# Gates for two output tiles at a time with the merge of the branches one chunk later, its additions on VectorE

## The chip, the cores and the metric

The kernel runs on one core of one Trainium2 chip. The metric is the device time of one execution in microseconds (us). Everything happens on the core's engines: TensorE (PE in the profile, its weight loads PEld), VectorE (DVE), ScalarE (ACT), GpSimd (POOL), and the queues that issue transfers (SP above all).

## The reference, cut to what matters

The program runs two blocks. The first has two "hybrid" layers, the second two layers of another attention and a mixture of experts. The change is in the first block only, in the step that merges three branches:

```python
def hybrid_layer(x, ...):                        # x: 256 tokens x 1024
    h = rmsnorm(x, norm1_w) * (1 + sc1) + sh1
    u = h @ w_in                                 # 1024 x 5632
    u_pool, u_conv, b_conv, c_conv, q, k, v, gate_logits = jnp.split(u, offsets, axis=-1)
    y_pool = pool_mixer(u_pool, pool_w, pool_scale)
    y_conv = b_conv * causal_short_conv(c_conv * u_conv, conv_w)
    ...                                          # y_attn: attention over q, k, v
    gates = jax.nn.sigmoid(gate_logits).reshape(B, S, N_BRANCH, D)   # 3 branches x 1024
    merged = (gates[:, :, 0] * (y_pool @ p_pool)
              + gates[:, :, 1] * (y_conv @ p_conv)
              + gates[:, :, 2] * (y_attn @ p_attn))
    x = x + g1 * (merged @ w_out)
    ...                                          # feed-forward part
```

All tensors are fp32.

## The kernel before

**Precision.** A matmul takes fp32r operands (a rounded form of fp32). To keep the accuracy each operand is held as a high and a low part, and a product is three matmuls: high by high, high by low, low by high. `split` (L267 to L281) makes the parts of a weight piece of 128 x 1024 values: ScalarE casts the high part (L278), VectorE subtracts it from the raw piece (L279). Three split buffers are used in turn. Activations keep both parts side by side, the high one in columns 0 to 255 and the low one in 256 to 511 (`hl`, `yhl`, `mhl`).

**Tiles.** Activations are held with features on the 128 partitions and 256 tokens along the row. `ws_tile` (L283 to L291) makes one output tile of 128 features: 8 weight pieces of 128 x 128, for each a matmul over 512 columns (L289) and one over 256 (L290). `fold` (L306) adds the two halves of the result: ScalarE copies one out, VectorE adds the other. `c_chunk` loads 256 columns of a weight matrix, so two output tiles; the loads go to the slots of a ring of 5, and a slot is free again when both its pieces are split. Results of matmuls land in four `mm` banks; temporaries of 512 columns (`t512`, `t` in the trace) are used in turn.

**The gates** (loop at L1037). Twelve chunks of 256 columns, in the order of the columns: all eight tiles of the pool branch, then the conv branch, then the attention branch. Each tile is a `ws_tile`, a `fold` and a tanh on ScalarE (L1045) into one of three buffers of eight tiles each. All 24 gate tiles are ready before the merge begins.

**The merge** (loop at L1056). Eight output tiles, two from each load of `p_pool`, `p_conv` and `p_attn`. A tile is 24 matmuls of 256 columns (L1067 to L1069) on the branch outputs `yhl`: 0 and 1 from the pool branch, 2 and 3 from the conv branch, 4 to 7 from attention. VectorE then multiplies the gates into the three results (L1071 to L1073), GpSimd adds the three (L1075, L1076; VectorE does it for the last two tiles), ScalarE writes the high part of the merged tile (L1077) and VectorE the low part (L1078). `w_out` follows (L1104 on); its first three tiles are done together and need three free `mm` banks (L300, L301).

**Work beside it.** TensorE's order is written by hand, the order in which the code issues. On the other engines a scheduler puts the instructions in an order by priority and readiness of what they need. `pump` runs the next piece of a list of steps (attention, then `pool_conv`, in layer 0 also products of small parameters, L673 on TensorE and L674 on VectorE); `finish` runs all that is left. `pool_conv` (from L992) makes `yhl` 0 to 3: per tile a matmul (L1021), the low part on VectorE (L1024), the convolution on VectorE (L1028, L1030), a product on GpSimd (L1031), the high part on ScalarE (L1032) and the low part on GpSimd (L1033). `finish` stands after gate chunk j = 3, so the last pieces of `pool_conv` are issued there. `pace` runs the products of `w_ada`, a matrix of the next modulation: on VectorE (L724, L726) or on ScalarE and GpSimd (L720, L722). Their sums go through TensorE; VectorE copies the result out of its bank (L682), TensorE transposes the copy (L685), and VectorE adds a bias (L686).

Of the kernel before, what the change touches and what calls it, by code (L numbers as in the profile page):

```python
# [20 lines left out]
P = 128  # L21
T = 256
D = 1024
KD = D // P
# [51 lines left out]
def kernel(ctx: ExitStack, tc: tile.TileContext, A, const, out):  # L76
    nc = tc.nc
    V, S, G, PE = nc.vector, nc.scalar, nc.gpsimd, nc.tensor
# [17 lines left out]
    def t512(dt=F32):  # L96
        return tmp.tile([P, 512], dt, tag="t", name=nm("t"))
# [4 lines left out]
    def mm_bank():  # L102
        return pmm.tile([P, 512], F32, tag="mm", name=nm("mm"))
# [64 lines left out]
    U_STATE, U_NAT, U_HL, U_YHL, U_SPLIT, U_PROB = 0, 14, (1, 2), (3, 4), (5, 6, 7), (15, 16)  # L168
# [8 lines left out]
    def unit(u, name, dt=F32):  # L177
        return units.tile([P, UNIT.get(u, 2048)], dt, tag=f"u{u}", name=nm(name))
# [54 lines left out]
    def wview(w, l, r0, r1, c0, c1):  # L233
        return w[l, r0:r1, c0:c1].rearrange("(k p) n -> p k n", p=P)
# [7 lines left out]
    def c_chunk(w, l, r0, r1, c):  # L242

        return raw(wview(w, l, r0, r1, c, c + 256), (r1 - r0) // P, 256)
# [20 lines left out]
    def split(src):  # L265
        key = (src.tensor.name, src.offset, str(src.ap))
        if key in early:  # L267
            return early.pop(key)
        k, n = src.shape[1], src.shape[2]
        u = unit(splits[nsplit[0] % len(splits)], "split", F32R)  # L270
        nsplit[0] += 1
        h = u[:, :k * n].rearrange("p (k n) -> p k n", k=k)
        lo = u[:, 1024:1024 + k * n].rearrange("p (k n) -> p k n", k=k)
        with ExitStack() as es:
            if held:
                for inst in held.pop():
                    es.enter_context(tc.issue_after(inst.ins))
            S.copy(h, src)  # L278
            V.tensor_sub(lo, src, h)  # L279
        return h, lo  # L280
# [289 lines left out]

    def attend(sets, ps, maskb, scale, E):

        rs = probs([(lhs, rhs, p[0]) for (lhs, rhs), p in zip(sets, ps)], maskb, 0, scale)
        for (p0, _), r in zip(ps, rs):
            for a in range(4):
                E[0].tensor_scalar_mul(p0[:, a], p0[:, a], r[:, a:a + 1])
        yield
# [300 lines left out]
    def block1(l, acc):  # L878
        W = A["w_in"]
# [62 lines left out]
            S.copy(vn[:, i], ps[i])  # L942

        yhl = HL(U_YHL, "yhl")
        gates = [unit(u, "gate")[:, :2048].rearrange("p (m t) -> p m t", m=8) for u in (8, 9, 10)]
        acc_v = gates[2].rearrange("p m t -> p (m t)")

        def attention():
            for j in range(2):
# [31 lines left out]
        for c in range(4):  # L981
            r = c_chunk(W, l, 0, D, 256 * c)
            for m in range(2):
                ps = ws_tile(r, m, hl)
                if c == 3:
                    c_ = t512()
                    done = fold(ps, c_[:, :T])
                    G.tensor_mul(zz[:, m, 2:], c_[:, :T], cu[:, m])
                else:
                    done = fold(ps, (up[:, m, 16:], cu[:, m], bc[:, m])[c])  # L990
# [44 lines left out]

        steps.append(pool_conv())

        for j in range(12):
            r = c_chunk(W, l, 0, D, 2560 + 256 * j)
            for m in range(2):  # L1040
                ps = ws_tile(r, m, hl)
                f = t512()
                done = fold(ps, f[:, :T])
                mm = 2 * j + m
                S.activation(gates[mm // 8][:, mm % 8], f[:, :T], AF.Tanh, scale=0.5)  # L1045
                pump()
                pace(*done)
            if j == 3:
                finish()
                acc_g = carve(unit(12, "acc"))  # L1050
                side[:] = [together(*side, ada_side(l, U_PROB, [(8, acc_g(512), 1), (9, acc_g(512), 2)], True))]
            if l == 0 and j == 4:
                params = load_parameters(carve(unit(14, "par")))
            if l == 0 and j == 7:
                steps.append(small_parameters(*params))
        mhl = HL(U_HL, "mhl")  # L1056
        for m in range(KD):
            if m % 2 == 0:
                r1 = slot().rearrange("p (k n) -> p k n", k=8)
                for w_, k0, k1 in (("p_pool", 0, 2), ("p_conv", 2, 4), ("p_attn", 4, 8)):  # L1060
                    nc.sync.dma_start(r1[:, k0:k1], wview(A[w_], l, 0, (k1 - k0) * P, m * P, m * P + 256))
            h1, l1 = split(r1[:, :, (m % 2) * P:(m % 2 + 1) * P])
            ba, bb = mm_bank(), mm_bank()
            regs = [ba[:, :T], ba[:, T:], bb[:, :T]]
            for br, (k0, k1) in enumerate(((0, 2), (2, 4), (4, 8))):
                for k in range(k0, k1):
                    PE.matmul(regs[br], h1[:, k], yhl[k][:, :T], start=k == k0, stop=False)  # L1067
                    PE.matmul(regs[br], h1[:, k], yhl[k][:, T:], start=False, stop=False)
                    PE.matmul(regs[br], l1[:, k], yhl[k][:, :T], start=False, stop=k == k1 - 1)  # L1069
            t0, t1 = t512(), t512()  # L1070
            V.scalar_tensor_tensor(t0[:, :T], gates[0][:, m], 1.0, regs[0], op0=OP.add, op1=OP.mult)  # L1071
            V.scalar_tensor_tensor(t0[:, T:], gates[1][:, m], 1.0, regs[1], op0=OP.add, op1=OP.mult)
            V.scalar_tensor_tensor(t1[:, :T], gates[2][:, m], 1.0, regs[2], op0=OP.add, op1=OP.mult)  # L1073
            E = G if m < KD - 2 else V
            E.tensor_add(t0[:, :T], t0[:, :T], t0[:, T:])  # L1075
            E.tensor_add(t0[:, :T], t0[:, :T], t1[:, :T])  # L1076
            done = (S.activation(mhl[m][:, :T], t0[:, :T], AF.Copy, scale=0.5),  # L1077
                    V.scalar_tensor_tensor(mhl[m][:, T:], t0[:, :T], 0.5, mhl[m][:, :T], op0=OP.mult, op1=OP.subtract))  # L1078
            pump()
            pace(*done)  # L1080

        while side:
            pace()
# [22 lines left out]
        for j in range(4):  # L1106
            r = wo[j] if j < 2 else c_chunk(A["w_out"], l, 0, D, 256 * j)
# [12 lines left out]
        for j in range(11):  # L1120
            rg, ru = wg if j == 0 else [c_chunk(A[w_], l, 0, D, 256 * j) for w_ in ("w_gate", "w_up")]
            early_ = ws_tiles(first, h2) if j == 0 else None
            for m in range(2):
# [7 lines left out]
                done = (V.tensor_mul(u_[:, :T], u_[:, :T], g_[:, :T]),)  # L1131
                k = 2 * j + m
# [9 lines left out]
        for j in range(4):  # L1142
            banks = [mm_bank() for _ in range(2)]
            for q, (k0, k1) in enumerate(((0, 8), (8, 16), (16, 22))):
                r = c_chunk(A["w_down"], l, k0 * P, k1 * P, 256 * j)
# [4 lines left out]
            for m in range(2):  # L1150
                done = residual(banks[m], 5, 2 * j + m, l + 1 < L)
# [9 lines left out]
    acc = norm_scale()  # L1161
    for l in range(L):
        acc = block1(l, acc)
# [582 lines left out]
    t = st[0][:, 1, 0:512]  # L1746
# [44 lines left out]
```

## Time and profile before

| | before |
|---|---|
| median of 3 runs | 1596.42 us (1595.8 to 1598.37) |
| the profiled execution's own time | 1598.5 us |
| its span in the trace | 1596.3 us |
| TensorE matmuls | 1508.8 us busy, 95% of the span |
| TensorE weight loads | 1091.9 us, 68% |
| VectorE | 977.2 us, 61% |
| ScalarE | 736.9 us, 46% |
| GpSimd | 251.3 us, 16% |
| granted TensorE clock, mean | 0.979 of full speed |

The profiled execution lies 2.1 us above the median, and 2.2 us of it lie outside its span. An engine's busy time counts its instructions from start to end; matmuls overlap, so a busy TensorE is the time in which at least one was under way. In the lists of single instructions the columns are start, duration, engine, line, operation, output<-input, the shapes, and in brackets the idle time of the engine before the instruction with the instruction that ended it.

### The profile page before, as it was taken

Reading aid. Unit: us, or ns where it says so; the run is one execution under the profiler, and the core shown is the slowest. Engines: PE = TensorE matmul, PEld = TensorE weight load, DVE = VectorE, ACT = ScalarE, POOL = GpSimd, SP = SyncE. Lnnn points to the kernel's source line nnn. Section 1 sums busy time; section 2 is a strip of 40 time slices with the busy share of each in tenths; the row PEclk is TensorE's granted clock in tenths of the full one; section 3 lists DMA queues with packets and bytes.
Section 4 is the critical chain, followed back from the end, with each engine's and each line's share of the span. In section 5 each row is a group of like instructions: output and inputs, shape, how many; then the busy total and the mean of one; then the engine's idle time right before and its main releaser. Section 6 shows DMA issues by size and latency. Waiting matters only on the chain. (4 is left out here: it accounts for less than half of the span.)

```text
span 1596.3 us, 24445 instructions
## 1 busy us (share of the span) xinstructions
PE 1508.8 (95%) x9211; PEld 1091.9 (68%) x9211; DVE 977.2 (61%) x1894; ACT 736.9 (46%) x1403; POOL 251.3 (16%) x279
## 2 busy tenths in 40 slices
PE   6999899999999999999998998999998999899996
PEld 5877788888887888888887876344436877344343
DVE  4769777777787767787657667222226776423224
ACT  3466745655446674566546565121115665211122
POOL 0333640001224263100003110000000310000000
PEclk9999999999999999999999998999998999899998
DMA  9666769656864675965535457999995648899995
GB/s 349 240 210 247 253 231 324 204 188 200 314 203 156 211 263 182 321 211 178 173 103 158 150 193 281 366 407 407 407 403 203 217 141 291 310 407 407 407 407 196
DMA packets 278476, 419.71 MB, mean 263 GB/s; under 512 B 12722, under 2 KB 147748, under 8 KB 278348
## 3 DMA queue, kind: packets, MB, share of 16 engines
q1 hardware_dynamic: 273052, 398.63, 70.6%
q0 software_dynamic: 5152, 19.14, 3.5%
q8 instruction: 77, 1.26, 0.3%
q14 instruction: 51, 0.42, 0.1%
q10 hardware_dynamic: 144, 0.26, 0.0%
HBM read 416.94 MB, written 1.05 MB: 262 GB/s over the span
## 5 line engine op out<-in xcount | busy, mean ns | idle before, releaser
L279 DVE TENSOR_TENSOR split<-raw,split 128x1024 fp32r<-128x1024 f32 (+4 forms) x330 | 412.6, 1254 | 113.1 <-ACT split L278 109.9
L289 PE MATMUL mm<-hl,split 128*128 128x512 f32 x1168 | 413.4, 397 | 0.0
L278 ACT CAST split<-raw 128x1024 fp32r<-128x1024 f32 (+4 forms) x330 | 328.8, 1000 | 130.0 <-PE mm L323 68.7
L290 PE MATMUL mm<-hl,split 128*128 128x256 f32 x1168 | 328.0, 281 | 0.6 <-DVE split L279 0.6
L289 PEld LDWEIGHTS mm<-hl,split 128*128 128x128 f32 x1168 | 219.5, 188 | 49.3 <-issue 0.9
L1597 PE MATMUL mm<-raw,xg 128*64 128x512 f32 x1024 | 233.6, 603 | 1.1 <-ACT xg L1564 1.1
L290 PEld LDWEIGHTS mm<-hl,split 128*128 128x128 f32 x1168 | 221.5, 190 | 1.1 <-DVE split L279 0.9
L1597 PEld LDWEIGHTS mm<-raw,xg 128*64 128x64 f32 x1024 | 70.2, 138 | 130.9 <-issue 113.1
L289 PE MATMUL mm<-ahl,split 128*128 128x512 f32 x352 | 123.4, 394 | 0.0
L306 ACT COPY t<-mm 128x256 f32<-128x256 f32 x152 | 56.7, 373 | 143.3 <-PE mm L290 133.4
L1597 PE MATMUL mm<-raw,t 128*64 128x512 f32 (+1 forms) x576 | 114.8, 549 | 1.5 <-ACT t L1643 1.4
L321 PE MATMUL mm<-split,hl 128*128 128x512 f32 (+4 forms) x272 | 102.1, 375 | 4.3 <-ACT split L278 3.2
L290 PE MATMUL mm<-ahl,split 128*128 128x256 f32 x352 | 98.7, 281 | 0.3 <-DVE split L279 0.3
L322 PE MATMUL mm<-split,hl 128*128 128x512 f32 (+4 forms) x272 | 96.0, 353 | 0.9 <-DVE split L279 0.8
L323 PE MATMUL mm<-split,hl 128*128 128x512 f32 (+4 forms) x272 | 96.2, 354 | 0.5 <-POOL hl L1210 0.4
L306 DVE TENSOR_TENSOR t<-mm,t 128x256 f32<-128x256 f32 x140 | 59.2, 423 | 49.5 <-ACT t L306 49.2
L1597 PEld LDWEIGHTS mm<-raw,t 128*64 128x64 f32 x576 | 39.4, 137 | 67.6 <-issue 50.8
L1673 DVE SCALAR_TENSOR_TENSOR t<-mm,s,t 128x512 fp32r<-128x512 f32 (+1 forms) x36 | 24.9, 691 | 91.8 <-ACT t L1672 91.8
L289 PEld LDWEIGHTS mm<-ahl,split 128*128 128x128 f32 x352 | 65.9, 187 | 15.0 <-ACT t L1095 0.2
L1672 ACT ACTIVATE t<-mm,s 128x512 fp32r<-128x512 f32 (+1 forms) x36 | 23.1, 640 | 106.0 <-PE mm L1597 106.0
L1643 ACT COPY t<-at 128x512 f32<-128x512 f32 x16 | 9.4, 588 | 129.9 <-PE at L1641 129.9
L290 PEld LDWEIGHTS mm<-ahl,split 128*128 128x128 f32 x352 | 66.5, 189 | 0.6 <-DVE split L279 0.6
(426 smaller groups left out, 2504.8 us busy)
## 6 DMA issues: line engine op xcount, KB each, us to landing
raw<-in_exp_w_gate_dram SPq DMA_DIRECT2D x128, 512.0 KB
raw<-in_exp_w_up_dram SPq DMA_DIRECT2D x128, 512.0 KB
raw<-in_exp_w_down_dram SPq DMA_DIRECT2D x128, 512.0 KB
raw<-in_w_in_dram SPq DMA_DIRECT2D x54, 1024.0 KB
raw<-in_w_ada_dram SPq DMA_DIRECT2D x30, 1024.0 KB
raw<-in_w_gate_dram SPq DMA_DIRECT2D x22, 1024.0 KB
raw<-in_w_up_dram SPq DMA_DIRECT2D x22, 1024.0 KB
ada<-in_w_ada_dram POOLq DMA_DIRECT2D x18, 1024.0 KB, 6.6
```

Source lines behind the costliest of these rows:

```text
L278: S.copy(h, src)
L279: V.tensor_sub(lo, src, h)
L289: PE.matmul(ps, h[:, k], x[k0 + k], start=first and k == 0, stop=False)
L290: PE.matmul(ps[:, :T], lo[:, k], x[k0 + k][:, :T], start=False, stop=last and k == K - 1)
L306: return S.copy(b[:, :T], ps[:, T:]), V.tensor_add(dst, ps[:, :T], b[:, :T])
L321: PE.matmul(ps[i][:, :n], xh, h[:, j], start=f, stop=False)
L322: PE.matmul(ps[i][:, :n], xh, lo[:, j], start=False, stop=False)
L323: PE.matmul(ps[i][:, :n], xl, h[:, j], start=False, stop=z)
L1597: PE.matmul(ps[64 * b:64 * b + 64, :], lhs(k, b), ws[k][b], start=k == 0, stop=k == nk - 1)
L1643: S.copy(aT, pb)
L1672: S.activation(yh[:, sl], pd_[:, :w], AF.Copy, scale=gs)
L1673: V.scalar_tensor_tensor(yl[:, sl], pd_[:, :w], gs, yh[:, sl], op0=OP.mult, op1=OP.subtract)
```

## The change

The twelve gate chunks go in another order: for a pair of output tiles (`pr`) the pool, the conv and the attention gates, then the next pair. A gate chunk is written to one of four places in a single buffer. The merge of a pair is a function, `merge(pr)`. It is called after the first gate chunk of the following pair (j = 3, 6, 9), and for the last pair after the loop. In a merge tile two of the three multiplications by the gates are joined into one over 512 columns; both additions are on VectorE in all tiles. The merged tiles and the `w_ada` sums lie in other buffers.

The diff, without the lines of buffers that only move and without the unchanged matmuls:

```diff
+        gates = unit(10, "gate").rearrange("p (s m t) -> p s m t", s=4, m=2)
+        def merge(pr):
...
+            r1 = slot().rearrange("p (k n) -> p k n", k=8)
...
+            s0 = 3 * pr % 4
+            two = (1, 2) if s0 == 3 else (0, 1)
+            one = 3 - sum(two)
+            for m in range(2):
+                h1, l1 = split(r1[:, :, m * P:(m + 1) * P])
...
+                V.scalar_tensor_tensor(t0.rearrange("p (b t) -> p b t", b=2), gates[:, s:s + 2, m], 1.0,
+                                       ba.rearrange("p (b t) -> p b t", b=2), op0=OP.add, op1=OP.mult)
+                V.scalar_tensor_tensor(t1[:, :T], gates[:, (s0 + one) % 4, m], 1.0, bb[:, :T], op0=OP.add, op1=OP.mult)
+                V.tensor_add(t0[:, :T], t0[:, :T], t0[:, T:])
+                V.tensor_add(t0[:, :T], t0[:, :T], t1[:, :T])
+                dst = mhl[2 * pr + m]
+                done = (S.activation(dst[:, :T], t0[:, :T], AF.Copy, scale=0.5),
+                        V.scalar_tensor_tensor(dst[:, T:], t0[:, :T], 0.5, dst[:, :T], op0=OP.mult, op1=OP.subtract))
+                pump()
+                pace(*done)
         for j in range(12):
-            r = c_chunk(W, l, 0, D, 2560 + 256 * j)
+            br, pr = j % 3, j // 3
+            r = c_chunk(W, l, 0, D, 2560 + 1024 * br + 256 * pr)
             for m in range(2):
...
-                S.activation(gates[mm // 8][:, mm % 8], f[:, :T], AF.Tanh, scale=0.5)
+                S.activation(gates[:, j % 4, m], f[:, :T], AF.Tanh, scale=0.5)
...
             if j == 3:
                 finish()
...
-            V.scalar_tensor_tensor(t0[:, :T], gates[0][:, m], 1.0, regs[0], op0=OP.add, op1=OP.mult)
-            V.scalar_tensor_tensor(t0[:, T:], gates[1][:, m], 1.0, regs[1], op0=OP.add, op1=OP.mult)
-            V.scalar_tensor_tensor(t1[:, :T], gates[2][:, m], 1.0, regs[2], op0=OP.add, op1=OP.mult)
-            E = G if m < KD - 2 else V
-            E.tensor_add(t0[:, :T], t0[:, :T], t0[:, T:])
-            E.tensor_add(t0[:, :T], t0[:, :T], t1[:, :T])
...
+            if br == 0 and pr:
+                merge(pr - 1)
+        merge(3)
```

In the changed kernel the numbers of lines are a few lower: `pool_conv`'s steps are L1020, L1023, L1027, L1029 (VectorE), L1030 and L1032 (GpSimd), L1031 (ScalarE); the merge's matmuls L1058 to L1060, its multiplications L1063 (two branches) and L1065, its additions L1066 and L1067, and the merged tile's parts L1069 and L1070.

**First place: TensorE in layer 0, at the last matmul of `pool_conv`** (`hl` is the input of the gates, `yhl` the branch outputs, `mm` and `at` are banks). Before:

```order
L290 MATMUL mm_1354<-hl_234,split_1351 128x256
L1021 MATMUL at_1381<-vn_228,up_230 128x256
L289 MATMUL mm_1398<-hl_233,split_1395 128x512
L290 MATMUL mm_1398<-hl_233,split_1395 128x256
L289 MATMUL mm_1398<-hl_233,split_1395 128x512
```

After:

```order
L290 MATMUL mm_1353<-hl_234,split_1350 128x256
L1020 MATMUL at_1380<-vn_228,up_230 128x256
L1058 MATMUL mm_1400<-yhl_687,split_1397 128x256
L1059 MATMUL mm_1400<-yhl_687,split_1397 128x256
L1060 MATMUL mm_1400<-yhl_687,split_1397 128x256
```

Behind that matmul stood a gate tile, and stands now the first merge tile, whose inputs `yhl` 1 to 3 are still to be finished from it and from the convolution.

**Second place: VectorE in layer 0, at the same spot**, from the low part of the pool branch on. Before:

```order
L1024 SCALAR_TENSOR_TENSOR yhl_687<-at_1381,cols,yhl_687 128x256
L1028 SCALAR_TENSOR_TENSOR t_1385<-up_230,cols,t_1385 128x256
L306 TENSOR_TENSOR t_1415<-mm_1398,t_1416 128x256
L1030 SCALAR_TENSOR_TENSOR t_1385<-up_230,cols,t_1385 128x256
L726 SCALAR_TENSOR_TENSOR gate_691<-ada_1061,cs,gate_691 128x512
```

After:

```order
L1023 SCALAR_TENSOR_TENSOR yhl_687<-at_1380,cols,yhl_687 128x256
L1027 SCALAR_TENSOR_TENSOR t_1384<-up_230,cols,t_1384 128x256
L279 TENSOR_TENSOR split_1481<-raw_1479,split_1481 128x1024
L1029 SCALAR_TENSOR_TENSOR t_1384<-up_230,cols,t_1384 128x256
L1063 SCALAR_TENSOR_TENSOR t_1426<-gate_1061,mm_1400 128x512
```

A `fold` between the two steps of the convolution has gone, a split of the next gate chunk stands there, and the merge's joined multiplication follows at once.

**Third place: VectorE in layer 1, at the copy of a `w_ada` sum in the merge** (L682; `mhl` is the merged tile). Before:

```order
L1071 SCALAR_TENSOR_TENSOR t_6182<-gate_4955,mm_6156 128x256
L1072 SCALAR_TENSOR_TENSOR t_6182<-gate_4956,mm_6156 128x256
L1073 SCALAR_TENSOR_TENSOR t_6183<-gate_4957,mm_6157 128x256
L279 TENSOR_TENSOR split_6242<-raw_6198,split_6242 128x1024
L279 TENSOR_TENSOR split_6284<-raw_6280,split_6284 128x1024
L1078 SCALAR_TENSOR_TENSOR mhl_6109<-t_6182,mhl_6109 128x256
L682 COPY t_6196<-at_6191 128x128
L1071 SCALAR_TENSOR_TENSOR t_6231<-gate_4955,mm_6205 128x256
L1072 SCALAR_TENSOR_TENSOR t_6231<-gate_4956,mm_6205 128x256
```

After:

```order
L1063 SCALAR_TENSOR_TENSOR t_6223<-gate_5300,mm_6197 128x512
L1070 SCALAR_TENSOR_TENSOR mhl_6152<-t_6186,mhl_6152 128x256
L1065 SCALAR_TENSOR_TENSOR t_6224<-gate_5300,mm_6198 128x256
L1066 TENSOR_TENSOR t_6223<-t_6223 128x256
L279 TENSOR_TENSOR split_6267<-raw_6238,split_6267 128x1024
L1067 TENSOR_TENSOR t_6223<-t_6223,t_6224 128x256
L279 TENSOR_TENSOR split_6294<-raw_6292,split_6294 128x1024
L1070 SCALAR_TENSOR_TENSOR mhl_6152<-t_6223,mhl_6152 128x256
L682 COPY t_6236<-at_6231 128x128
L279 TENSOR_TENSOR split_6319<-raw_6292,split_6319 128x1024
L306 TENSOR_TENSOR t_6260<-mm_6243,t_6261 128x256
```

The copy still stands behind two splits and the low part of a merged tile; two additions of that tile have come into the row before it. On TensorE the transpose of the copy (L685) has one tile of 16 matmuls between it and the product that fills the bank; before it was one merge tile.

## Rows read from the trace of the kernel before

**Rows 1.** Busy time by stretch (bounds, length, engines, PEclk, DMA share, GB/s).

```profile
134.20:187.20 53.00, 50.41 (x293) 42.40 (x292) 44.98 (x70) 38.18 (x70) 25.66 (x21) 0.97 0.70 237
187.20:218.20 31.00, 26.73 (x207) 25.45 (x205) 23.68 (x40) 13.93 (x20) 18.30 (x16) 0.94 0.61 195
542.24:587.40 45.16, 45.16 (x266) 39.42 (x265) 29.28 (x40) 35.77 (x67) 21.61 (x17) 1.00 0.71 241
587.40:618.70 31.30, 26.91 (x205) 25.35 (x203) 26.10 (x42) 15.78 (x23) 19.72 (x16) 0.95 0.62 210
```

**Rows 2.** Waits of TensorE: engine, line, releaser; total us, times, longest.

```profile
...
PE at L685 <- DVE t L682: 6.5, 4, 3.4
...
PE mm L300 <- DVE t L1072: 2.1, 2, 1.3
...
PE mm L1069 <- DVE split L279: 1.6, 2, 1.4
...
PE at L673 <- DVE rwb L674: 1.3, 2, 0.9
...
PE mm L1067 <- DVE t L306: 0.7, 1, 0.7
...
PE mm L1067 <- DVE t L1072: 0.6, 1, 0.6
...
```

**Rows 3.** TensorE in order of time, both layers (start, duration, instruction, idle before).

```profile
196.26 0.28 PE L1069 MATMUL mm<-yhl,split 128*128 128x256 f32 x1
...
198.87 0.33 PE L685 MATMUL at<-con,t 128*128 128x128 f32 x1 [2.33 <-DVE t L682]
...
601.51 0.33 PE L685 MATMUL at<-con,t 128*128 128x128 f32 x1 [3.37 <-DVE t L682]
```

**Rows 4.** GpSimd, ScalarE and VectorE in order of time, ahead of 198.87.

```profile
196.12 1.58 POOL L1076 TENSOR_TENSOR t<-t,t 128x256 f32<-128x256 f32 x1
...
197.74 0.42 ACT L1077 ACTIVATE mhl<-t 128x256 fp32r<-128x256 f32 x1 [2.35 <-POOL t L1076]
...
198.19 0.43 DVE L1078 SCALAR_TENSOR_TENSOR mhl<-t,mhl 128x256 fp32r<-128x256 f32 x1 [1.06 <-ACT mhl L1077]
198.53 0.28 DVE L682 COPY t<-at 128x128 f32<-128x128 f32 x1
...
199.39 1.22 DVE L279 TENSOR_TENSOR split<-raw,split 128x1024 fp32r<-128x1024 f32 x1
200.53 0.41 DVE L1073 SCALAR_TENSOR_TENSOR t<-gate,mm 128x256 f32<-128x256 f32 x1
```

**Rows 5.** Stretches after short and long waits; columns as in rows 1.

```profile
200.10:203.60 3.50, 3.50 (x19) 3.50 (x18) 2.43 (x5) 0.53 (x2) 2.69 (x2) 0.52 0.57 180
203.60:207.00 3.40, 3.40 (x31) 3.40 (x30) 2.74 (x5) 0.97 (x2) 2.34 (x2) 1.00 0.92 299
843.90:848.70 4.80, 4.78 (x21) 4.77 (x21) 2.19 (x5) 3.24 (x6) 0.17 (x1) 0.50 0.00 0
```

**Rows 6.** The chain to the last inputs of the merge, layer 0 then layer 1.

```profile
136.68 0.48 DVE L1024 SCALAR_TENSOR_TENSOR yhl<-at,cols,yhl 128x256 fp32r<-128x256 f32 x1
...
141.34 0.53 POOL L423 MEMSET par<- 128x512 f32 x1
...
544.65 1.65 DVE L279 TENSOR_TENSOR split<-raw,split 128x1024 fp32r<-128x1024 f32 x1
546.22 0.47 DVE L1024 SCALAR_TENSOR_TENSOR yhl<-at,cols,yhl 128x256 fp32r<-128x256 f32 x1
...
547.22 0.48 DVE L1030 SCALAR_TENSOR_TENSOR t<-up,cols,t 128x256 f32<-128x256 f32 x1
...
547.78 0.74 POOL L1031 TENSOR_TENSOR t<-t,vn 128x256 f32<-128x256 f32 x1 [0.88 <-DVE t L1030]
...
548.55 0.41 ACT L1032 CAST yhl<-t 128x256 fp32r<-128x256 f32 x1 [0.91 <-POOL t L1031]
...
549.04 1.17 POOL L1033 TENSOR_TENSOR yhl<-t,yhl 128x256 fp32r<-128x256 f32 x1 [0.52 <-ACT yhl L1032]
```

More of the change, by code (lines that the diff above doesn't have):

```diff
@@ L944, in block1 @@
         yhl = HL(U_YHL, "yhl")
-        gates = [unit(u, "gate")[:, :2048].rearrange("p (m t) -> p m t", m=8) for u in (8, 9, 10)]
-        acc_v = gates[2].rearrange("p m t -> p (m t)")
+        acc_v = unit(9, "acc")
         def attention():
@@ L1036, in block1 @@
         steps.append(pool_conv())
+        gates = unit(10, "gate").rearrange("p (s m t) -> p s m t", s=4, m=2)
+        mhl = []
+        def merge(pr):
+            if pr % 2 == 0:
+                mh = unit((8, 9)[pr // 2], "mhl", F32R).rearrange("p (k n) -> p k n", n=512)
+                mhl.extend(mh[:, k] for k in range(4))
+            r1 = slot().rearrange("p (k n) -> p k n", k=8)
+            for w_, k0, k1 in (("p_pool", 0, 2), ("p_conv", 2, 4), ("p_attn", 4, 8)):
+                nc.sync.dma_start(r1[:, k0:k1], wview(A[w_], l, 0, (k1 - k0) * P, 256 * pr, 256 * pr + 256))
+            s0 = 3 * pr % 4
[3 more added lines that the diff above has]
+                h1, l1 = split(r1[:, :, m * P:(m + 1) * P])
+                ba, bb = mm_bank(), mm_bank()
+                regs = {two[0]: ba[:, :T], two[1]: ba[:, T:], one: bb[:, :T]}
+                for br, (k0, k1) in enumerate(((0, 2), (2, 4), (4, 8))):
+                    for k in range(k0, k1):
+                        PE.matmul(regs[br], h1[:, k], yhl[k][:, :T], start=k == k0, stop=False)
+                        PE.matmul(regs[br], h1[:, k], yhl[k][:, T:], start=False, stop=False)
+                        PE.matmul(regs[br], l1[:, k], yhl[k][:, :T], start=False, stop=k == k1 - 1)
+                t0, t1 = t512(), t512()
+                s = (s0 + two[0]) % 4
+                V.scalar_tensor_tensor(t0.rearrange("p (b t) -> p b t", b=2), gates[:, s:s + 2, m], 1.0,
[8 more added lines that the diff above has]
+                pace(*done)
         for j in range(12):
-            r = c_chunk(W, l, 0, D, 2560 + 256 * j)
+            br, pr = j % 3, j // 3
+            r = c_chunk(W, l, 0, D, 2560 + 1024 * br + 256 * pr)
             for m in range(2):
@@ L1043, in block1 @@
                 done = fold(ps, f[:, :T])
-                mm = 2 * j + m
-                S.activation(gates[mm // 8][:, mm % 8], f[:, :T], AF.Tanh, scale=0.5)
+                S.activation(gates[:, j % 4, m], f[:, :T], AF.Tanh, scale=0.5)
                 pump()
@@ L1055, in block1 @@
                 steps.append(small_parameters(*params))
[L1056 to L1070, printed above, removed]
-            V.scalar_tensor_tensor(t0[:, :T], gates[0][:, m], 1.0, regs[0], op0=OP.add, op1=OP.mult)
-            V.scalar_tensor_tensor(t0[:, T:], gates[1][:, m], 1.0, regs[1], op0=OP.add, op1=OP.mult)
-            V.scalar_tensor_tensor(t1[:, :T], gates[2][:, m], 1.0, regs[2], op0=OP.add, op1=OP.mult)
-            E = G if m < KD - 2 else V
-            E.tensor_add(t0[:, :T], t0[:, :T], t0[:, T:])
-            E.tensor_add(t0[:, :T], t0[:, :T], t1[:, :T])
[L1077 to L1080, printed above, removed]
+            if br == 0 and pr:
+                merge(pr - 1)
+        merge(3)
         while side:
```

## The prediction

> **What bounds the kernel now.** I read the page first: TensorE is busy for 95% of the span, so the time is TensorE's matmuls, the stretches in which they run at the lower clock, and the gaps between them. The change adds and removes no matmul (12 gate chunks and 8 merge tiles of 24 stay), so everything follows from gaps and clock. Next I read the table of stretches [rows 1]: the gates have hardly a gap in layer 1 (45.16 us busy of 45.16) and 2.6 us in layer 0; the merges have 4.3 (31.00 less 26.73) and 4.4 us. VectorE is the next engine: 23.7 us in the merge of layer 0, 26.1 in layer 1, of 31, and about 65 to 85% in the gates. Then I read who ends TensorE's gaps [rows 2]: the largest item is L685, the transpose of a `w_ada` sum, 6.5 us in 4 waits. Two of them, 2.33 and 3.37 us, stand in the two merges [rows 3]; 0.8 us stand elsewhere. The chain before the first of them shows why [rows 4]: GpSimd's second addition (1.58 us) lets ScalarE write the high part, that lets VectorE write the low part (idle 1.06 us before it), and the copy that TensorE waits for stands behind it. Last I read what a wait does to the clock [rows 5]: in the 3.50 us after the 2.33 us wait the granted clock was 0.52, near the lower level of 1.2 GHz, and 19 matmuls ran; in the next 3.40 us it was 1.00 and 31 ran, 0.11 us each. The drop so cost 3.50 - 19 x 0.11 = 1.4 us, 0.4 per us. A stretch of 4.80 us at 0.50, later in the trace, thus cost 1.9 us.
>
> **What the change removes.**
> - GpSimd's additions leave the chain of rows 4, so the two long waits at L685 lose their cause: 2.33 + 3.37 = 5.7 us.
> - The waits of the first matmuls of a merge tile, for banks and splits (L1067 and L1069: 0.7 + 0.6 + 1.6 = 2.9 us) [rows 2], come from merge tiles that follow each other at TensorE's pace. With four to six gate tiles between pairs VectorE catches up: a gate tile holds it for a split and an addition, 1.22 us and 0.43 (the low part's row, of the same shape), and at most a `w_ada` product of twice the columns, of 45.16 / 16 = 2.8 us of TensorE [rows 1, 4]. All 2.9 us go.
> - `w_out`'s first tiles wait for banks behind the last two merge tiles (L300, 2.1 us in 2) [rows 2]. The last merge now follows two gate tiles and comes in with VectorE ahead; I leave 0.2 us, gain 1.9.
> - The clock: the granted clock was 0.94 and 0.95 in the merges and 0.97 in the gates of layer 0 [rows 1], one drop of the kind of rows 5 in each (a 3.5 us drop at half clock is 0.06 of 31 us). The two behind L685 go with their waits; the one at the head of the gates in layer 0 falls into the new wait below and is counted there. 3 x 1.4 = 4.2 us.
> - Each wait also holds up the pipeline when it ends: from the matmul at 196.26 to the one at 198.87 are 2.61 us, of which 2.33 are called wait and 0.11 is the usual step, so about 0.15 is left [rows 3, 5]. Eight such waits go and about four come: 0.6 us.
>
> Together 5.7 + 2.9 + 1.9 + 4.2 + 0.6 = 15.3 us.
>
> **What it adds.**
> - *The merge's inputs are late.* `merge(0)` is called right after the chunk behind which `finish` issues the last piece of `pool_conv`. Before, 16 gate tiles lay between that and the first merge tile, 45 us or more [rows 1], and hid it entirely; this cover is gone. TensorE is at the first merge tile where its gate tile began, at 134.20 in layer 0 and 542.24 in layer 1 [rows 1], and can do 10 of the 24 matmuls (1.1 us) before it needs the last inputs. Layer 0: VectorE ends the pool branch's low part at 136.68 + 0.48 = 137.16 [rows 6]; then in its new order the first convolution step (0.48, as the second), a split (1.22 alone, 1.65 beside GpSimd [rows 4, 6]; 1.5 taken, as GpSimd works in part of it), the second step (0.48): 139.6. GpSimd's product 0.74 and a handover of 0.08: 140.4; ScalarE's cast 0.41: 140.9; meanwhile GpSimd clears a buffer (0.53), and then its subtraction [rows 6]. That took 1.17 beside a split; here VectorE's next instruction waits for TensorE, so I take the product's 0.74: 141.7. The wait is 141.7 - 134.2 - 1.1 = 6.4 us. Layer 1: the order up to the second convolution step is that of before, so 547.22 + 0.48, + 0.08 + 0.74, + 0.03 + 0.41, + 0.08 + 0.74 = 549.8 [rows 6]; less 542.24 and 1.1, 6.5 us. Together **12.9 us**; with the split at 1.22 or 1.65 and the subtraction at 1.17 the ends are 12.5 and 14.0.
> - The same rows bear on a rule of the Trainium skill ("SBUF — State Buffer", section "SBUF: two separate sides"): VectorE with two inputs in SBUF and GpSimd share a pair of ports, and whoever starts first holds it for the whole instruction. The rows agree: the split took 1.22 us or 1.65, GpSimd 0.74 or 1.17, by 0.43 apart in both. By the rule the sum stays as it is; were the two slowed by halves instead, each layer's chain would end some 0.2 us later and the sum would be 4.1 us.
> - *The clock after these waits.* They are far longer than the 2.33 us that drew 0.52 [rows 5]. I price each by the longest stretch seen, 1.9 us: 3.8 us. From below the price is 0 (no drop), from above I know none larger than 1.9 but leave 2.3.
> - *The copy in layer 1.* L682 now stands behind the second tile of `merge(2)`: joined multiplication (at most 2 x 0.41), single one 0.41, two additions and the low part (0.43 each, the low part's row), two splits of 1.22, copy 0.28 [rows 4]: 5.2 us by durations, some 0.1 less for each overlap, 4.6. TensorE has one gate tile of 2.8 us in that time, so it waits 1.8. In layer 0 no tile's low part stands so; 0.2. Together 2.0 us; ends 0.5 and 3.4, the latter being the wait of today.
> - *The small parameters in layer 0.* L673 waits for VectorE's L674, 1.3 us in 2 [rows 2]. One of these pairs now falls beside a merge tile's multiplications (0.82 + 0.41 [rows 4]): 0 to 1.4 us more, 0.7 taken.
> - Additions on VectorE: 24 more (12 in each layer) of about 0.43 us less the joined multiplications' saving. VectorE has 31.00 - 23.68 = 7.3 and 5.2 us to spare in the merges and more in the gates [rows 1]; TensorE's work per pair (6 gate tiles and 2 merge tiles, some 22 us) hides it. Nothing, else up to 1 us a layer.
> - Behind the merges: the ring's slots come free a little earlier and with them loads of the next stage; -0.4, ends -1 and +1.5 (a cast for `w_out` that stands before ScalarE's parts of the merge).
>
> Together 12.9 + 3.8 + 2.0 + 0.7 - 0.4 = 19.0 us. Net **+3.7 us**.
>
> **The forecast.** The profiled execution of 1598.5 us becomes 1602.2; its 2.1 us above the median are outside the argument, so on the median: 1596.4 + 3.7 = **1600.1 us**.
>
> **The rivals.**
> - *A: the clock does not fall behind the new waits* (matmuls before them keep it, as 10 of them run inside the wait). 1600.1 - 3.8 = 1596.3, no change: this is the other side. For it: waits of 1.4 us [rows 2] left no drop that the merges' 0.94 and 0.95 would show; against: the 2.33 us one did. It decides where the clock stays at 1.00 behind `merge(0)`.
> - *B: the long wait gives time back.* While TensorE stands, ScalarE and VectorE split ahead, and the later short waits vanish: the 2.0 and 0.7 added ones, and the 0.8 at L685 and 1.3 at L673 that stay in the sum. 1600.1 - 4.8 = 1595.3, no change. Against it: only three split buffers, so the lead is two tiles.
> - *A and B together*: 1591.5, faster.
> - *C: the added middle waits each draw a drop*, at the copy in layer 1, L673 in layer 0 and one behind `merge(0)`'s second tile: 3 x 1.4 = 4.2, 1604.3. It decides where a wait of 1.5 to 2 us is followed by a clock near 0.5; rows 5 show it for 2.33.
> - *D: the change doesn't reorder TensorE as it says.* The order of TensorE is written by hand, so I give this nothing.
>
> **How the numbers follow.** About 0.2%, 3.2 us, is what a measurement of this kernel can tell from no change: faster is below 1593.2, slower above 1599.6. The forecast has 0.38 (its own spread of some 2.5 us, from the bounds of the copy, L673, the loads and the chain, puts 0.22 of it above 1599.6), A 0.15 and B 0.15 (each 0.03 faster, 0.12 same), A with B 0.10 (faster), C 0.17 (slower), and 0.05 for a surprise (0.04 slower). Faster 0.16, same 0.41, slower 0.43. The range leaves out half of A with B below and the end of C above: 1592.5 to 1605.
>
> **What would show it.** In the trace of the changed kernel: at the first merge tile of either layer TensorE stops for 6 to 7 us in all, ended by GpSimd's L1032 or ScalarE's L1031; the clock behind it is near 0.5 for 3 to 5 us; no L685 wait above 2 us; the waits at the first matmuls of merge tiles and at L300 near zero; GpSimd's additions gone. The prediction is wrong if the inputs of `merge(0)` come with less than 4 us of wait, if the clock stays up, or if VectorE, with its additions, becomes late for gate tiles too.

## The result and the profile after

| | before | after |
|---|---|---|
| median of 5 runs | 1598.37 us (1595.8 to 1598.89) | 1607.48 us (1606.92 to 1613.48) |
| ratio to before | | 1.0065, 95% interval 1.0052 to 1.0079 |
| profiled execution, span | 1598.5, 1596.3 us | 1606.92, 1605.1 us |
| granted TensorE clock, mean | 0.979 | 0.974 |

The change makes the kernel slower, by some 10 us (9.1 by the medians, 10.4 by the ratio, 8.8 by the spans). The forecast was slower by 3.7 us, with a range that ended at 1605.0: the sign was right, the size was not. Of the 7.4 us between the forecast median of 1600.1 and 1607.5, 2.0 are the base, which is 1598.4 over five runs where the prediction had 1596.4 from three; the other 5.4 are the change.

The head of the page shows that no engine got new work to speak of. GpSimd lost 24 instructions and 27 us, VectorE's sum is the same (its 24 new additions of 0.42 us make some 10 us; the 280 large splits took 9.9 us less in sum, 1292 ns each instead of 1327, and the joined multiplications save 2.3), and TensorE is busy 6 us longer with the same number of matmuls, so some ran at the lower clock:

```profile
span 1605.1 us, 24376 instructions
PE 1515.1 (94%) x9211; PEld 1095.3 (68%) x9211; DVE 977.8 (61%) x1902; ACT 735.8 (46%) x1403; POOL 223.9 (14%) x255
```

The table of stretches answers to [rows 1]. The columns are bounds, length, busy time and count of TensorE, its weight loads, VectorE, ScalarE, GpSimd, the granted clock, the DMA share and GB/s. The first line of each pair is the first merge pair (48 matmuls) of a layer, the second all that follows up to `w_out`:

```profile
133.08:146.96 13.88, 10.23 (x50) 8.70 (x49) 9.69 (x21) 4.13 (x8) 4.51 (x5) 0.63 0.27 86
146.96:221.56 74.60, 68.55 (x446) 59.80 (x445) 61.15 (x100) 47.49 (x81) 25.75 (x18) 0.98 0.73 246
544.42:558.89 14.47, 10.69 (x49) 9.40 (x49) 9.21 (x16) 4.91 (x10) 3.32 (x4) 0.65 0.27 88
558.89:628.23 69.34, 65.64 (x421) 58.20 (x419) 50.59 (x75) 46.44 (x78) 23.31 (x16) 0.98 0.74 249
```

A merge pair without gaps at the upper clock takes 5.76 us (2 x 2.88, as the later pairs of this kernel do). The first one took 13.88 and 14.47 us, at a granted clock of 0.63 and 0.65. Its gaps on TensorE in layer 0, with the wait just ahead of it, then in layer 1, in order of time (a matmul takes 0.28 us at the upper clock, and one that runs alone at the lower one 0.58):

```profile
132.73 0.70 PE L1020 MATMUL at<-vn,up 128*128 128x256 f32 x2 [2.40 <-DVE vn L1016]
...
134.28 0.58 PE L1058 MATMUL mm<-yhl,split 128*128 128x256 f32 x1 [0.51 <-ACT yhl L1022]
136.09 0.58 PE L1059 MATMUL mm<-yhl,split 128*128 128x256 f32 x1 [1.22 <-DVE yhl L1023]
138.27 0.58 PE L1059 MATMUL mm<-yhl,split 128*128 128x256 f32 x1 [0.98 <-POOL yhl L1032]
139.79 0.58 PE L1058 MATMUL mm<-yhl,split 128*128 128x256 f32 x1 [0.73 <-ACT yhl L1031]
140.60 0.58 PE L1059 MATMUL mm<-yhl,split 128*128 128x256 f32 x1 [0.22 <-POOL yhl L1032]
...
545.46 0.39 PE L1059 MATMUL mm<-yhl,split 128*128 128x256 f32 x1 [0.66 <-DVE yhl L1023]
...
547.99 0.58 PE L1058 MATMUL mm<-yhl,split 128*128 128x256 f32 x1 [2.02 <-ACT yhl L1022]
550.88 0.58 PE L1058 MATMUL mm<-yhl,split 128*128 128x256 f32 x1 [0.80 <-ACT yhl L1031]
551.68 0.58 PE L1059 MATMUL mm<-yhl,split 128*128 128x256 f32 x1 [0.22 <-POOL yhl L1032]
```

The waits themselves add up to 3.7 us in each layer, far less than the 6.4 and 6.5 forecast. But the matmuls between them fill the rest, most of them at the lower clock, and the tile is late by the whole chain: its last input comes 140.60 - 133.08 = 7.5 us after its first matmul in layer 0 and 551.68 - 544.42 = 7.3 in layer 1. The granted clock was 0.50 from 134.3 to 144.5 in layer 0, and from 547.3 to 557.5 in layer 1.

The waits of TensorE over the whole run, which answer to [rows 2] (engine, line, releaser; total, times, longest):

```profile
PE at L685 <- DVE t L682: 5.6, 5, 2.2
...
PE at L673 <- DVE rwb L674: 4.1, 2, 2.8
```

No wait at the first matmul of a later merge tile or at L300 is left in the list, and those waits were 5.0 us before [rows 2]. But the transposes of the `w_ada` sums still wait 5.6 us (6.5 before), now behind gate tiles, and the small parameters 4.1 (1.3 before).

**Where the time went**, from the starts of the stages' first matmuls in both traces, both layers together:

| stage | forecast | measured |
|---|---|---|
| the later merge pairs (in before: the excess of all pairs over 2.88 us a tile) | -12.0 | -14.7 |
| first tiles of `w_out` | -1.9 | -2.9 |
| the first merge pair, excess over 5.76 us | +16.7 | +16.8 (8.1 and 8.7) |
| the gate tiles with the transposes and small products among them | +1.3 | +11.0 |
| elsewhere | -0.4 | -1.4 |
| together | +3.7 | +8.8 |

Two rows are off: the gates by 9.7 us, and the merges by 2.7 the other way. (0.9 us of each is two `w_ada` products and their transposes that merely moved from the merges among the gate tiles.)

**What holds up the gates.** The longest wait, 2.85 us, stands before the second product of a small-parameter pair. VectorE must read the first (L674), and that stands behind a `fold` that waits for ScalarE, where a `w_ada` product waits for its transfer. TensorE, VectorE and ScalarE in order of time:

```profile
191.57 0.49 PE L673 MATMUL at<-rwg,ones 128*128 128x128 f32 x2 [2.85 <-DVE rwb L674]
...
190.89 0.42 DVE L306 TENSOR_TENSOR t<-mm,t 128x256 f32<-128x256 f32 x1 [2.52 <-ACT t L306]
191.23 0.28 DVE L674 TENSOR_REDUCE rwb<-at 128x16 f32<-128x128 f32 x1
...
188.85 1.33 ACT L720 ACTIVATE t<-ada,cs 128x512 f32<-128x512 f32 x2 [2.28 <-DMA ada<-in_w_ada_dram]
190.09 0.35 ACT L306 COPY t<-mm 128x256 f32<-128x256 f32 x1
```

The transposes wait in the same way. In layer 1 the copy at 598.47 stands behind two splits that wait for ScalarE's casts, and the casts stand behind `w_ada` products there. At 613.49 it stands behind a merge tile and two splits, as the prediction had it for this one place. VectorE from the last tile's multiplications to that copy, without a gap:

```profile
608.95 0.67 DVE L1063 SCALAR_TENSOR_TENSOR t<-gate,mm 128x512 f32<-128x512 f32 x1
...
610.55 1.21 DVE L279 TENSOR_TENSOR split<-raw,split 128x1024 fp32r<-128x1024 f32 x1
611.68 0.41 DVE L1067 TENSOR_TENSOR t<-t,t 128x256 f32<-128x256 f32 x1
612.02 1.21 DVE L279 TENSOR_TENSOR split<-raw,split 128x1024 fp32r<-128x1024 f32 x1
613.16 0.41 DVE L1070 SCALAR_TENSOR_TENSOR mhl<-t,mhl 128x256 fp32r<-128x256 f32 x1
613.49 0.28 DVE L682 COPY t<-at 128x128 f32<-128x128 f32 x1
```

TensorE's waits were 2.23 us at the first and 1.43 at the second. After the waits of 2.85 and 2.23 us the granted clock fell; the table of stretches there (columns as above):

```profile
191.80:195.30 3.50, 3.50 (x14) 2.99 (x14) 2.02 (x3) 1.19 (x2) 3.23 (x3) 0.57 0.68 218
598.90:602.40 3.50, 3.50 (x13) 3.04 (x14) 1.81 (x3) 3.50 (x7) 3.34 (x3) 0.57 1.08 381
```

The gate tiles there took 4.43 and 4.22 us instead of 2.8, the price of [rows 5]. After the waits of 1.43 and 1.48 us the next tiles took 2.90 and 2.97, so those drew no drop.

### The profile page after: what moved, and what is told of

It reads as the page before. It is cut to its first block, busy times and chain, and to the rows that moved or that the text cites. A ratio compares the mean times of both kernels' runs of the same rounds, so it can differ in the third digit from the quotient of the medians.

```text
span 1605.1 us, 24376 instructions
## 1 busy us (share of the span) xinstructions
PE 1515.1 (94%) x9211; PEld 1095.3 (68%) x9211; DVE 977.8 (61%) x1902; ACT 735.8 (46%) x1403; POOL 223.9 (14%) x255
## 5 line engine op out<-in xcount | busy, mean ns | idle before, releaser
L279 DVE TENSOR_TENSOR split<-raw,split 128x1024 fp32r<-128x1024 f32 (+4 forms) x330 | 402.8, 1224 | 114.5 <-ACT split L278 110.9
```

## The experiments

Ratios are to runs of the kernel before on the same chip, with 95% intervals. The edits are of the changed kernel ("after") unless another is named; the kernels with the transposes behind or the additions edited have line numbers a few off. One profile was taken of each kernel. The changed stages in it, from the first matmul behind `pool_conv` to the first of `w_out`, both layers together:

| kernel | us |
|---|---|
| before | 159.2 |
| after | 172.3 |
| the later merge | 156.3 |
| additions back on GpSimd | 175.9 |
| before, additions on VectorE | 151.6 |
| transposes two tiles behind | 171.0 |
| two banks | 169.7 |
| both repairs | 163.8 |
| before, both repairs | 157.2 |
| before, both repairs, additions on VectorE | 153.6 |
| copies on ScalarE | 169.5 |
| later merge, both repairs | 149.5 |
| the same, copies on ScalarE | 149.7 |

The rest of the span, in which at most the first tiles of `w_out` are touched, took 1432.8 to 1440.8 us, so several us of a difference in time can come from there.

### The merge one gate chunk later still

```diff
-        gates = unit(10, "gate").rearrange("p (s m t) -> p s m t", s=4, m=2)
+        gates = unit(8, "gate").rearrange("p (s m t) -> p s m t", s=5, m=2)
...
-            if br == 0 and pr:
+            if br == 1 and pr:
                 merge(pr - 1)
```

> The changed kernel with each merge called one gate chunk later still (after j = 4, 7, 10; a ring of five gate places instead of four). If the late inputs of the first merge tile are the main cost (that tile and the next took 8.1 us too long in layer 0 and 8.7 in layer 1 of the changed kernel's trace), two more gate tiles (5.6 us) now cover the chain of 7.2 to 7.5 us: some 0.8 us of wait stay per layer and no drop of the clock, so about 15 us less than the changed kernel's 1607.5: 1592 to 1594. If the cost is VectorE with its additions, the wait moves to the next tiles and the time stays above 1602.

Ratio 0.9967 (0.9956 to 0.9977), median 1594.0: 15.7 us less than the changed kernel by the ratios, as expected from the late inputs, and faster than the kernel before. The first pair in both layers (table of stretches):

```profile
139.64:146.54 6.90, 6.02 (x51) 5.82 (x49) 6.90 (x14) 3.30 (x6) 2.10 (x4) 1.00 0.45 164
544.16:550.98 6.82, 6.02 (x50) 5.81 (x49) 5.99 (x9) 3.30 (x6) 1.59 (x2) 1.00 0.46 154
```

6.90 and 6.82 us instead of 13.88 and 14.47, and no drop of the clock, although TensorE's wait ahead of the stage is still there in layer 0:

```profile
133.46 0.70 PE L1020 MATMUL at<-vn,up 128*128 128x256 f32 x2 [2.39 <-DVE vn L1016]
```

This settles the largest term: 14.6 of the 16.8 us are the place of the first merge. The gates still have waits at the transposes, one of 4.2 us.

### The additions back on GpSimd

```diff
-                V.tensor_add(t0[:, :T], t0[:, :T], t0[:, T:])
-                V.tensor_add(t0[:, :T], t0[:, :T], t1[:, :T])
+                E = G if pr < 3 else V
+                E.tensor_add(t0[:, :T], t0[:, :T], t0[:, T:])
+                E.tensor_add(t0[:, :T], t0[:, :T], t1[:, :T])
```

> The changed kernel with the additions of the first six merge tiles back on GpSimd. If VectorE's 24 more additions make it late (rival), the time falls by 3 to 5 us, to 1603. If they are covered and shorten the chain to the copy that TensorE waits for (my theory), the waits at the transposes behind merge tiles grow by 1 to 1.5 us each where they fall on such a tile (1.48 and 1.43 us in the changed kernel) and perhaps draw a drop of the clock: 1608 to 1612.

Ratio 1.0108 (1.0089 to 1.0128): slower still by 0.4%, some 7 us, more than I expected; 3.6 us of it stand in the changed stages of the profile. The rival, that VectorE with its additions is late, is refuted. The waits at the two transposes I had named grew by 0.4 and 0.3 us (to 1.89 and 1.69), not by 1 to 1.5; a wait of 3.58 us came at a small product. The low part of a merged tile now waits for ScalarE and GpSimd, and VectorE, in order, holds back the splits and the read of the small product behind it:

```profile
203.24 0.43 DVE L1071 SCALAR_TENSOR_TENSOR mhl<-t,mhl 128x256 fp32r<-128x256 f32 x1 [1.88 <-ACT mhl L1070]
...
205.64 0.28 DVE L674 TENSOR_REDUCE rwb<-at 128x16 f32<-128x128 f32 x1
...
205.98 0.49 PE L673 MATMUL at<-rwg,ones 128*128 128x128 f32 x2 [3.58 <-DVE rwb L674]
```

### The kernel before with its additions on VectorE

```diff
-            E = G if m < KD - 2 else V
+            E = V
```

> The kernel before with all additions of the merge on VectorE, order unchanged. The prediction's step held GpSimd's additions to be the cause of the two waits at L685 (2.33 and 3.37 us, each with a drop of 1.4 us): then 8 us go, 1589. The rival from the changed kernel's trace: the copy is late since it stands on VectorE, in order, behind splits that wait for ScalarE; then 1 to 1.5 us of each wait stay away and at most the drops with them: 2 to 5 us less, 1592 to 1596.

Ratio 0.9971 (0.9960 to 0.9982): 4.6 us less than before, in the band of the rival. The waits at L685 in the merges fell from 2.33 and 3.37 us to 1.90 and 1.11 instead of vanishing, and new waits of 1.4 and 2.5 us came at `w_out`'s first tiles, for splits. In the changed stages 7.6 us went, close to the 8 of the first theory, and the granted clock stayed at 1.00 in them, where it fell three times before. One of these three drops, some 1.4 us, can't be put down to the additions: it followed the wait ahead of the gates, 2.41 us before and 2.40 here. So GpSimd's additions were a part of those two waits, and how much of the time is theirs stays open.

### The transposes two tiles behind

A transpose waits in a list; `pump` runs it at the next tile. Here it runs at the second; `lag` is on from the gates to the end of the merges.

```diff
-        while posts:
+        while posts and (not lag[0] or posts[0] in aged):
             posts.pop(0)()
+        aged[:] = posts
```

> The changed kernel with the transpose of each w_ada sum two tiles behind its product on TensorE instead of one, in the gates and merges of both layers. If the copy L682 is late only by its place in VectorE's order, the four waits (0.34, 1.48, 2.23, 1.43 us) and one drop of the clock (1.4 us) go: 7 us less than 1607.5, 1600 to 1601. If VectorE is late as a whole, the wait moves to the next tile's matmuls and the time stays within 2 us of 1607.

Ratio 1.0045 (1.0030 to 1.0061): 3.2 us less than the changed kernel by the ratios, half of what the first theory gives. The two intervals overlap, the changed stages are 1.3 us shorter, and the median of 1606.9 lies in the band of the second, so a gain is not shown. All four waits at the transposes are gone, but TensorE then waits at the small products for longer, 5.5 us instead of 4.1 (one line later in this file):

```profile
PE at L674 <- DVE rwb L675: 5.5, 2, 3.6
```

By the trace both theories have a part: the place in VectorE's order makes the copy late, and much of the time that is saved there is lost at the next thing that needs VectorE.

### The small products in two banks

```diff
-            pb = at_bank()
-            for o, src, dst in ((0, rb, rwb), (KD * N_EXP, rwg[:, l], rws)):
-                v = pb[:, o:o + KD * N_EXP]
+            for src, dst in ((rb, rwb), (rwg[:, l], rws)):
+                v = at_bank()[:, :KD * N_EXP]
```

> The changed kernel with the two matmuls of each pair of small-parameter products (L673) in two banks, so that the second no longer waits for VectorE to read the first. If that wait (2.85 and 1.29 us, and a drop of the clock of some 1.6 us behind the longer) is a cost of its own, 5 to 6 us go: 1601 to 1603. If VectorE is simply late there, the wait moves to the next transpose or gate tile and less than 2 us go.

Ratio 1.0049 (1.0031 to 1.0067): 2.6 us less by the ratios and in the changed stages, half of what was expected, and the interval overlaps that of the changed kernel. The waits at L673 are gone; those at the transposes grew from 5.5 to 7.3 us in the two layers.

### Both repairs

> The changed kernel with both repairs, the transposes of the w_ada sums two tiles behind and the small-parameter products in two banks. What then remains against the kernel before is the late inputs of the first merge tile (16.8 us with the clock) less what the change removes. By the waits and drops in the changed kernel's trace 5.5 + 1.4 + 4.1 + 1.6 = 12.6 us go: 1595. If the waits only move from one to the next, above 1602.

Ratio 1.0016 (1.0006 to 1.0027): 7.8 us less than the changed kernel by the ratios. No wait is left at a transpose or a small product, but 2.6 us came up in layer 0 at gate tiles that wait for a split, and 1.5 in layer 1 at tiles that wait for splits. So of the gates' 11.0 us about 8 are waits for small pieces of VectorE's work that can be moved, and the rest is VectorE and ScalarE late with their splits. What remains against before is the first merge pair less the gain in the other merges.

### Both repairs on the kernel before

> The kernel before with the two repairs alone, no reordering of the gates and no additions moved. Its waits at L685 (6.5 us) and L673 (1.3 us) and two drops of the clock (2.8 us) go if the place of the copy in VectorE's order is all: 9 to 11 us less than before, 1588 to 1590 on a before of 1598 to 1600. If GpSimd's additions hold up the merge in another way (a bank, a buffer), the waits move to the merge's matmuls and less than 5 us go.

Ratio 1.0012 (0.9999 to 1.0025): no gain at all, against 9 to 11 us expected. The waits at L685 and L673 are gone, and the merge's own matmuls wait instead: the later tiles, five of eight in each layer, take 4.0 to 4.7 us each, one after the other. The changed stages are 2.0 us shorter, but the rest of the span is 2.1 longer. The loop that sets this pace, VectorE first, then GpSimd, then ScalarE (line numbers one higher than before):

```profile
604.16 0.42 DVE L1072 SCALAR_TENSOR_TENSOR t<-gate,mm 128x256 f32<-128x256 f32 x1
604.49 0.41 DVE L1073 SCALAR_TENSOR_TENSOR t<-gate,mm 128x256 f32<-128x256 f32 x1
604.82 0.42 DVE L1074 SCALAR_TENSOR_TENSOR t<-gate,mm 128x256 f32<-128x256 f32 x1
...
605.23 1.58 DVE L280 TENSOR_TENSOR split<-raw,split 128x1024 fp32r<-128x1024 f32 x1
607.88 0.43 DVE L1079 SCALAR_TENSOR_TENSOR mhl<-t,mhl 128x256 fp32r<-128x256 f32 x1 [1.08 <-ACT mhl L1078]
608.23 0.42 DVE L1072 SCALAR_TENSOR_TENSOR t<-gate,mm 128x256 f32<-128x256 f32 x1
...
604.99 0.74 POOL L1076 TENSOR_TENSOR t<-t 128x256 f32<-128x256 f32 x1 [1.65 <-DVE t L1073]
605.80 1.60 POOL L1077 TENSOR_TENSOR t<-t,t 128x256 f32<-128x256 f32 x1
...
607.43 0.42 ACT L1078 ACTIVATE mhl<-t 128x256 fp32r<-128x256 f32 x1 [2.71 <-POOL t L1077]
```

From one L1072 to the next are 4.07 us: three multiplications, the two additions on GpSimd, the high part on ScalarE, the low part on VectorE, and only then the next tile's multiplications, since VectorE runs in order. VectorE idles 1.08 us in each turn and TensorE waits for it. The trace of the kernel before suggests that the same delay was there, paid at one long wait behind a transpose, which let VectorE catch up; no run shows that by itself.

### Both repairs on the kernel before, additions on VectorE

> The kernel before with both repairs and all additions of the merge on VectorE. With the repairs alone the merge tiles took 4.1 us each, in a loop from VectorE through GpSimd's two additions (0.74 and 1.60 us) and ScalarE back to VectorE, which idles 1.07 us in it. If that loop sets the pace, a tile falls to VectorE's own work of some 3.1 us and 10 us go against the repairs alone: 1589 to 1592. If VectorE's work as such sets it, the additions make the tile longer and the time rises to 1601 or more.

Ratio 0.9966 (0.9949 to 0.9982): 7.4 us less than the repairs alone by the ratios, though the two intervals are wide; 10 were expected. The loop is gone, most merge tiles take 2.9 to 3.7 us. One tile in each layer takes 6.6 to 7.1, with a wait of 2.4 and 2.5 us for a split and the drop of the clock behind it (the waits in layer 0):

```profile
PE mm L1070 <- DVE split L280: 2.7, 2, 2.5
```

VectorE is now short of time in a merge that runs in one piece: 27.19 us busy of 29.57 in layer 1. The repairs add nothing to the additions: those alone gave 0.9971 and the shorter stages (151.6 us against 153.6).

### The copies on ScalarE

```diff
-        V.tensor_copy(m, ps[:, :P])
+        S.copy(m, ps[:, :P])
```

> The changed kernel with the copies L682 on ScalarE instead of VectorE. If VectorE's order (merge tile, splits) makes the transposes late, their waits (5.5 us and one drop of 1.4) fall by half or more and L673's by nothing: 1602 to 1604. If the copies are late on any engine in order, since ScalarE has the w_ada products and casts in front too, the time stays at 1606 to 1609.

Ratio 1.0059 (1.0040 to 1.0079), the same as the changed kernel within the intervals. The waits at the transposes are 5.9 us, one of them 3.6, while those at the small products fell from 4.1 to 1.8. ScalarE is no better a place; its casts, products and copies stand in order just as VectorE's work does, which fits, but no run takes that apart.

### The later merge with both repairs, without and with the copies on ScalarE

> The merge one gate chunk later still, with both repairs. From the trace of the later merge alone (1594, waits at the transposes of 5.9 and 1.2 us, at L673 0.8, one drop of the clock of about 1.3 us) some 8 to 9 us go: 1585 to 1587, 0.8% below the kernel before. If VectorE is late as a whole, 1590 or more.

> The later merge with both repairs and the copies L682 on ScalarE. One wait of 1.6 us at a transpose is left without it; if it goes, 1 to 2 us less than the 0.9942 of that kernel: a ratio of 0.993 to before. If ScalarE's casts come later by it, 0.995 or more.

Ratio 0.9942 (0.9923 to 0.9961), median 1588.6, profiled span 1583.5 us: 0.6% faster than the kernel before, the fastest of all. It is somewhat less than expected (0.992), since 2.6 us of waits for splits came up in the merge of layer 0 and one wait of 1.6 us stayed at a transpose:

```profile
PE mm L1061 <- DVE split L280: 2.6, 2, 1.7
...
PE at L685 <- DVE t L682: 1.6, 1, 1.6
```

With the copies on ScalarE it is 0.9954 (0.9935 to 0.9972), no better.

**What the new order itself is worth** is not shown by this. The rival is a single line in the kernel before, its additions on VectorE: 0.9971, against 0.9967 for the later merge, which has them there too. With both repairs on both sides it is 0.9966 (0.9949 to 0.9982) in the old order and 0.9942 (0.9923 to 0.9961) in the new one; the intervals overlap, and the changed stages are 4.1 us shorter in the new one, 153.6 against 149.5.

## Why the prediction was right in part and wrong in sum

- **The late inputs of the first merge tile: right, in size and cause.** 12.9 us of wait and 3.8 of clock were forecast, 16.8 measured. The chain ended 7.5 and 7.3 us after the tile's start, by the prediction 7.5 and 7.6. Less the 1.1 us of the ten matmuls this makes 6.4 and 6.2 us; the remaining 1.7 and 2.5 us are the clock, so the two terms were right too. Two of the prediction's signs were not: TensorE's recorded waits are 3.7 us in each layer, not 6 to 7, and so under the 4 us that were to speak against it. The clock had fallen inside the chain, and the matmuls in it, slower, took the place of waiting. The later merge shows the cause: two gate tiles in between take 14.6 us of it away.
- **What leaves the merges: right in size, one cause wrong.** -14.7 and -2.9 us instead of -12.0 and -1.9. GpSimd's additions do set the pace of the merge, but through the loop of 4.1 us per tile that the repaired kernel before laid bare, and not only by delaying one copy: with that copy out of the way nothing was gained (ratio 1.0012).
- **The step that failed: "the two long waits at L685 lose their cause", and the 2.0 and 0.7 us set against it.** The waits lost their place and a part of their cause, not all of it. A transpose has one tile on TensorE between the product and itself, and the copy between them stands in VectorE's order behind whatever the scheduler puts there. I followed the new order for one such copy, in layer 1 (1.8 us forecast, 1.43 measured), and gave the other three 0.2 us together; they were 0.34, 1.48 and 2.23 us, the last of them against the sign that no wait at L685 lies above 2 us. The copy with 1.48 stands behind a `fold`, that with 2.23 behind two splits, and both wait for ScalarE, which has `w_ada` products in front. L673 was 2.85 us more instead of 0.7: the pair beside the merge tile waited 1.29, within its bounds, but the other pair, given nothing more than before, waited 2.85. Of the 9.7 us that the gates are off, L685 has 2.8, L673 2.1, two drops of the clock 3.0, the two moved products 0.9; the rest is small. The rows for it were there in [rows 2]: 0.8 us of L685's waits and all of L673's stood in the gates, which I read as small remains and not as the sign of a queue without slack.
- **The drops of the clock.** I let three go and added two. Two more came, behind the waits of 2.23 and 2.85 us, 1.4 and 1.6 us each. That is rival C's mechanism, partly at other places and behind longer waits; C put it behind waits of 1.5 to 2 us, and those of 1.43 and 1.48 drew none.
- **Rival A is refuted:** the clock was at 0.50, its lower level of 1.2 GHz, for some 10 us in each layer. In layer 0 it fell 1.5 us after the wait of 2.40 us ahead of the tile and before the tile's own longer waits; that same drop stood at the head of the gates in the kernel before. **Rival B,** that the long wait gives time back to the later tiles, is not seen: the small waits grew.
- **VectorE's additions cost nothing,** as forecast. Back on GpSimd they cost 7 us more, 3.6 of it in the changed stages.
- **What stays open:** 16 gate tiles of layer 1 took 2.83 us instead of 2.77, some 0.8 us, without a wait in the trace. No run tells why.

The forecast in the sum: with the gates' term at what it measured, 11.0 instead of 1.3, the same sum gives 13.4; the larger gain in the merges and elsewhere brings it to 8.8.

## What to carry to other kernels

When work is moved to fill gaps, look first at where its inputs end: the call was one chunk too early for a chain of 7.5 us, and one chunk later turned 0.65% slower into 0.3% faster. Then test the simplest part of the change alone: one line in the old order, the additions on VectorE, gave the same 0.3%. A wait names who came last, not what would be late next: take the named wait away in a copy of the kernel, without the change, before counting it as gain. On engines that run in order every small copy or reduction that TensorE waits for after one tile is at risk from any reordering, so give it two tiles or a bank of its own together with the change; both together were worth 7.8 us here, and nothing in the kernel before, where another loop set the pace.

## What the runs showed of the hardware that I had not expected

The two slow operations in the loop are slow together. GpSimd's second addition takes 1.60 us beside a split and the split 1.58 beside GpSimd; alone they take 0.74 and 1.21. The Trainium skill ("SBUF — State Buffer", section "SBUF: two separate sides") says that VectorE with two inputs in SBUF and GpSimd hold their shared ports one after the other, for a whole instruction. The rows agree: GpSimd's addition at 605.80 begins beside a split that began at 605.23 and ends at 607.40, 0.59 us after the split's end at 606.81, most of the 0.74 us that it takes alone. This fits the shorter splits of the changed kernel, and makes the additions on VectorE, 0.41 us each, cheaper for both engines than on GpSimd.

The length of a wait alone does not tell whether the clock falls. It fell behind waits of 2.23, 2.33, 2.43 and 2.85 us, and did not behind 1.43, 1.48 and 1.67. But one of 1.89 us drew a drop (additions back on GpSimd: the next gate tile took 4.53 us), one of 1.90 us drew none (the kernel before with its additions on VectorE: the next merge tile took 2.94), and one of 2.22 us drew none (two banks, at a transpose in layer 1). The clearest case is the wait at the last matmul of `pool_conv` in layer 0, 2.39 to 2.41 us in every kernel. In the kernel before, where gate tiles follow, the granted clock fell to 0.50 some 1.5 us after it; in the six other kernels where gate tiles follow it stayed at 1.00. Before, then the later merge:

```profile
133.85 0.70 PE L1021 MATMUL at<-vn,up 128*128 128x256 f32 x2 [2.41 <-DVE vn L1017]
...
135.47 0.63 PE L289 MATMUL mm<-hl,split 128*128 128x512 f32 x1
...
133.81 0.58 PE L289 MATMUL mm<-hl,split 128*128 128x512 f32 x1
...
135.75 0.40 PE L289 MATMUL mm<-hl,split 128*128 128x512 f32 x1
```

Where the first merge tile follows with its short waits, in all six kernels of that kind, it fell each time. What decides is not shown; a single drop in one trace, some 1.4 us, is therefore a weak base for a term of a sum.
